# A chunked recurrence beside attention: first products that wait for a whole group, and PSUM banks split by kind

## The chip, the cores and the metric

The kernel runs on one core of a Trainium2 chip. The metric is the device time of one execution in microseconds (us). The engines of the core are TensorE (PE; its weight loads are listed as PEld), VectorE (DVE), ScalarE (ACT), GpSimd (POOL) and SyncE (SP), which issues nearly all transfers. Each engine works through its own queue in order; semaphores tie the queues together.

## The reference, cut to what matters

One layer of a backbone with two parallel head groups on 1024 latent and 256 context tokens: differential attention (8 heads) and an RWKV-7 recurrence over 16 heads of size 64 in both directions. Their gated outputs go through one output projection and a final norm.

```python
def step(S, inp):                      # S: heads x value x key
    r_t, w_t, k_t, v_t, kk_t, b_t = inp
    sa = jnp.einsum('bhvk,bhk->bhv', S, -kk_t)
    S = S * w_t[:, :, None, :] + sa[..., None] * b_t[:, :, None, :] + v_t[..., None] * k_t[:, :, None, :]
    return S, jnp.einsum('bhvk,bhk->bhv', S, r_t)

# attention, for each block of 128 queries
p = jax.nn.softmax(s, axis=-1)         # two maps, m = 0 and 1
a = p[:, :, 0] - lam * p[:, :, 1]
o = jnp.einsum('bhqk,bkhv->bqhv', a, v)
```

## The kernel before

A first phase computes the input projection and writes its results to scratch tensors in HBM; the change doesn't touch it. The function `mix_phase` does the rest: the recurrence, the attention and the output projection run side by side, and after the recurrence's end the tail finishes attention and projection.

The recurrence is computed in chunks of 32 tokens (`CH`). One step of the outer loop, a tick, is one chunk for four pairs of heads in both directions. There are 80 ticks: ten items (a group of four pairs times five segments of 256 tokens) of eight chunks. Two chunks (`HN`) make a part, so there are 40 parts. The four pairs are handled as two duos `w`. For each duo and for odd and even parts there is a buffer `L` (left operands) and `R` (right operands: state, values and a solved part).

A tick in `step` is: first products (line 893) into PSUM, which are copied (line 901) into rows 96 to 128 of `R`; state products (line 913), which are multiplied with the decay (line 924) into the next chunk's state rows of `R`; output products (line 936), which are copied (line 939) into `ys` and stored to HBM by `store_y` (line 953). Duo `w` has bank `bank[w]`, with columns 0 to 128 for the first products, 128 to 256 for the outputs and 256 to 512 for the states. After the first products comes `fill(0)`, after the outputs `fill(1)`: these calls put attention work and, a piece each, the norms, the projections and the next item's inverse into the program.

`load_part` loads the operands of a later part when the part two before it has been read: L<-kt (line 772), R<-vb (781), L<-ra (782), and the inverse Tb<-td (793). `prep` (products at 803, copies at 806) multiplies the loaded operands with the inverse and writes the result into rows 96 to 128 of `L`; it is written in the second tick of the part before, for one duo after the other, through one bank `yb`. The inverse itself is computed by `inverse` on POOL (lines 734 and 736), from `aw`, and goes to HBM as `td`.

Attention is a generator: `scores` (1057, 1060) writes negated score blocks and running minima, an exponential follows the last block (1068), `weight` (1074, 1075) and `combine` (1081) mix the two maps, `trans` (1089, 1091) transposes and `values` (1104) multiplies with the values. PSUM tiles for the scores and the transposes have two buffers each. `norm` (980 to 1007) normalises the recurrence's outputs, `load_wo` (1247 to 1251) loads and splits the projection's weights, `project` (1275 to 1300) multiplies.

The order of the instructions on each engine isn't that of the program. A planner simulates the program, and whenever an engine is free it takes, of what is ready by its own estimate, the instruction that is earliest in the program; inside `tc.high_priority(offset=n)` an instruction counts as n places earlier. That order is then fixed, and on the chip every engine keeps to it. Before, only the copies at 901 and the multiplications at 924 have an offset (`HPC = 500`).

Of the kernel before, what the change touches and what calls it, by code (L numbers as in the profile page):

```python
# [34 lines left out]
NC = SEG // CH  # L35
HN = 2
# [11 lines left out]
YBUF = 1  # L48
# [14 lines left out]
HPY = 0  # L63
# [677 lines left out]
def mix_phase(ctx, tc, i, o, s, ident, nhalf, dram, td0, neglam, subg, lnh, heads, psm):  # L741
# [94 lines left out]
    bank = [psx.tile([P, 512], F32, name=f"bank{w}") for w in duos]  # L836
# [18 lines left out]
    def start_item(w, m):  # L855
# [6 lines left out]
        px = bank[w]  # L862
# [18 lines left out]

    def step(j, k, fill):
# [4 lines left out]
        for w in duos:  # L887
            L, R = slots[w, j % 2]
            for d in range(2):
                for e in range(2):  # L890
                    for h in range(2):
                        u = 64 * e + 32 * h
                        nc.tensor.matmul(bank[w][u:u + 32, 64 * d:64 * d + 64], L[0:96, e, h, d, k, 96:128],
                                         R[0:96, k, d, e, hv(h)], start=True, stop=True, tile_position=(0, u))
        with ahead(HPC):
            for w in duos:
                R = slots[w, j % 2][1]
                for e in range(2):
                    for h in range(2):
                        u = 64 * e + 32 * h  # L900
                        (nc.vector.tensor_copy if w else nc.scalar.copy)(  # L901
                            R[96:128, k, :, e, hv(h)], bank[w][u:u + 32, 0:128].rearrange("p (d v) -> p d v", d=2))
        later_prep = k == HN - 1 and j + 1 < n_part
        if later_prep:
            prep(j + 1, 0, yb)
        fill(0)
        for w in duos:
            L, R = slots[w, j % 2]
            for e in range(2):
                for d in range(2):  # L910
                    for h in range(2):
                        o_ = 256 + 128 * d + 64 * e
                        nc.tensor.matmul(bank[w][hv(h), o_:o_ + 64], L[:, e, h, d, k, 0:64],  # L913
                                         R[:, k, d, e, hv(h)], start=True, stop=True, tile_position=(0, 64 * h))
        with ahead(HPC):
            for w in duos:
# [6 lines left out]
                for h in range(2):  # L923
                    nc.vector.tensor_tensor(dst[:, :, :, hv(h)], bank[w][hv(h), 256:512].rearrange("p (d e v) -> p d e v", e=2, d=2),  # L924
                                            wcs[p0][hv(h), 2 * w:2 * w + 2, sg + 1, :, c:c + 1].rearrange("p e d o -> p d e o").broadcast_to([HD, 2, 2, HD]), op=ALU.mult)
        g = c // 4
        if c % 4 == 0:
            ysb[m, g] = cp.tile([P, 4, NL, HD], F32, tag="ys", name=f"ys{m}_{g}", bufs=YBUF)
        for w in duos:
            L, R = slots[w, j % 2]  # L930
            for e in range(2):
                o_ = P + 64 * e
                for h in range(2):
                    for d in range(2):
                        q = 64 * d + 32 * h
                        nc.tensor.matmul(bank[w][q:q + 32, o_:o_ + 64], L[:, e, h, d, k, 64:96], R[:, k, d, e, hv(h)],  # L936
                                         start=True, stop=True, tile_position=(0, q))
        for w in duos:
            nc.scalar.copy(ysb[m, g][:, c % 4, 2 * w:2 * w + 2], bank[w][:, P:2 * P].rearrange("p (e v) -> p e v", e=2))
        if later_prep:  # L940
            prep(j + 1, 1, yb)
# [101 lines left out]
    def attention():  # L1043
# [128 lines left out]
        for n in range(NB + 2):  # L1172
# [25 lines left out]
            if pp is not None:  # L1198
                vp = [(pp, c) for c in range(1 if len(st[pp]["ch"]) > 1 else 0, len(st[pp]["ch"]))]
# [348 lines left out]
```

## Time and profile before

| what | value |
|---|---|
| median of three runs | 2613.61 us (2607.57 to 2620.56) |
| the profiled execution | 2612.43 us |
| its span, first to last instruction | 2610.6 us |
| mean granted TensorE clock | 0.943 |
| TensorE busy | 2363.7 us |

The profile is that of one execution. For each group of instructions of a line it has the busy time, the mean duration and what ended the idle time before them; for each engine it lists who it waited for. A timeline row gives start and length of neighbouring instructions of one line, merged. The granted clock is given as a share of 2.4 GHz; TensorE has two levels, 2.4 and 1.2 GHz. Starting times are counted from the span's start. The mixed phase begins at about 1230 us; the recurrence's products run until about 2383 us.

### The profile page before, as it was taken

The numbers are of one execution on the slowest core, as the hardware profiler recorded it, in microseconds if no ns is written. First come the engines' busy times: TensorE is split into PE (matmuls) and PEld (weight loads), VectorE is DVE, ScalarE is ACT, GpSimd is POOL, SyncE is SP. The second block draws the span as 40 slices with busy tenths as digits, with TensorE's granted clock in tenths as the row PEclk, the third lists the DMA queues.
The fourth block names the chain that finished last, engine by engine and source line by source line (L and its number), as shares of the span: only waits on it lengthen the run. The fifth ranks groups of instructions, "written<-read, shape, count | busy, mean of one in ns | idle before, by whom it ended". The sixth has DMA issues, their size and how long they took to land.

```text
span 2610.6 us, 60873 instructions
## 1 busy us (share of the span) xinstructions
PE 2363.7 (91%) x23907; PEld 1902.6 (73%) x23907; DVE 1559.8 (60%) x3210; ACT 1192.9 (46%) x2606; POOL 1166.5 (45%) x1725
## 2 busy tenths in 40 slices
PE   6999999999999999898698989898989998898796
PEld 4888888888888888787466767676766676776674
DVE  5656565555455655533566877685745565576558
ACT  3334443334334343331466666574545554564342
POOL 4234343243433342465446666556647311043564
PEclk9999999999999999998799999897988998999898
DMA  7465656565646564567978887877887888787445
GB/s 240 108 157 134 178 143 181 139 164 161 155 128 161 135 180 120 165 167 165 225 156 166 163 163 146 165 150 169 167 200 183 211 191 190 176 222 207 148 146 181
DMA packets 516734, 437.56 MB, mean 168 GB/s; under 512 B 156552, under 2 KB 460852, under 8 KB 511329
## 3 DMA queue, kind: packets, MB, share of 16 engines
q1 hardware_dynamic: 514352, 427.94, 66.8%
q0 software_dynamic: 2096, 5.75, 1.2%
q8 instruction: 188, 3.08, 0.5%
q14 instruction: 98, 0.79, 0.1%
HBM read 258.69 MB, written 163.86 MB: 162 GB/s over the span
## 4 chain that ended last, share of the span: by engine, by line
PE 55%; DMA 19%; DVE 8%; POOL 6%; SPq 5%; issue 3%; ACT 2%; POOLq 0%; DVEq 0%; ACTq 0%
DMA L<-kt 5%; PE sc L1057 5%; PE po L1104 4%; PE bank L913 3%; PE pa L1089 3%; PE yb L803 3%; PE pg L449 3%; DMA acc<-acc 2%; PE pso L1298 2%; DMA wst<-w_out 2%; PE pso L1299 1%; DMA Tb<-td 1%; PE pso L1300 1%; PE bank L936 1%; PE psg_v L335 1%
## 5 line engine op out<-in xcount | busy, mean ns | idle before, releaser
L1057 PE MATMUL sc<-ka,q 128*128 128x512 f32 (+1 forms) x832 | 302.3, 452 | 17.5 <-DVE pb L1060 9.3
L1060 DVE TENSOR_SCALAR_CACHE_REDUCE pb<-sc,mn 128x512 f32<-128x512 f32 x256 | 191.6, 749 | 112.2 <-PE sc L1057 104.4
L1068 ACT ACTIVATE pb<-pb,mn 128x1536 f32<-128x1536 f32 (+1 forms) x160 | 218.4, 1365 | 75.3 <-DVE pb L1060 74.5
L734 POOL TENSOR_TENSOR tmp<-aw,tt 128x31 f32<-128x31 f32 (+15 forms) x310 | 163.4, 527 | 168.9 <-DMA aw<-kt 67.8
L1104 PE MATMUL po<-vk,aT 128*128 128x128 f32 x1600 | 237.2, 289 | 0.9 <-ACT aT L1091 0.7
L1104 PEld LDWEIGHTS po<-vk,aT 128*128 128x128 f32 x1600 | 217.2, 201 | 17.2 <-ACT aT L1091 1.4
L479 POOL TENSOR_SCALAR ta<-ta,ka 128x256 f32<-128x256 f32 x80 | 81.1, 1014 | 292.8 <-DVE bk L477 292.7
L456 ACT COPY km<-ptk 64x256 f32<-64x256 f32 x320 | 117.4, 367 | 182.3 <-PE ptk L453 160.4
L736 POOL TENSOR_TENSOR tt<-tt,tmp 128x31 f32<-128x31 f32 (+15 forms) x310 | 180.8, 583 | 18.2
L803 PE MATMUL yb<-L,Tb 32*32 32x96 f32 x2496 | 105.3, 269 | 81.1 <-DMA L<-kt 59.5
L806 ACT COPY L<-yb 32x384 f32<-32x384 f32 x312 | 146.3, 469 | 67.9 <-PE yb L803 63.8
L1057 PEld LDWEIGHTS sc<-ka,q 128*128 128x128 f32 x832 | 137.8, 201 | 53.6 <-DVE pb L1060 20.1
L1081 DVE SCALAR_TENSOR_TENSOR pb<-pb,cc,pb 128x512 f32<-128x512 f32 (+1 forms) x208 | 167.8, 856 | 2.0
L1091 ACT COPY aT<-pa 128x512 f32<-128x512 f32 (+1 forms) x208 | 116.2, 570 | 104.0 <-PE pa L1089 102.2
L924 DVE TENSOR_TENSOR R<-bank,wc 64x256 f32<-64x256 f32 x312 | 130.9, 420 | 54.6 <-PE bank L913 45.3
L450 DVE TENSOR_TENSOR km<-pg,msk 128x512 f32<-128x512 f32 x80 | 55.1, 688 | 175.7 <-PE pg L449 147.0
L1089 PE MATMUL pa<-ident,pb 128*128 128x128 f32 x800 | 137.7, 297 | 17.6 <-DVE acc L1292 10.4
L803 PEld LDWEIGHTS yb<-L,Tb 32*32 32x32 f32 x2496 | 66.3, 114 | 116.2 <-issue 42.2
L1060 DVE TENSOR_SCALAR_CACHE_REDUCE pb<-sc 128x512 f32<-128x512 f32 (+1 forms) x160 | 101.3, 636 | 80.7 <-PE sc L1057 67.8
L913 PEld LDWEIGHTS bank<-R,L 128*64 128x64 f32 x2560 | 102.2, 152 | 49.1 <-issue 20.5
L913 PE MATMUL bank<-R,L 128*64 128x64 f32 x2560 | 126.2, 244 | 8.3 <-ACT R L901 4.3
L1089 PEld LDWEIGHTS pa<-ident,pb 128*128 128x128 f32 x800 | 97.2, 150 | 45.1 <-DVE acc L1292 13.1
(354 smaller groups left out, 6496.2 us busy)
## 6 DMA issues: line engine op xcount, KB each, us to landing
kt<-km SPq DMA_DIRECT2D x160, 256.0 KB
L<-kt SPq DMA_DIRECT2D x80, 512.0 KB
acc<-acc SPq DMA_DIRECT2D x50, 512.0 KB
ra<-ra SPq DMA_DIRECT2D x160, 128.0 KB
L<-ra SPq DMA_DIRECT2D x80, 256.0 KB
R<-vb SPq DMA_DIRECT2D x160, 64.0 KB
y<-ys SPq DMA_DIRECT2D x80, 128.0 KB
yn<-y SPq DMA_DIRECT2D x40, 256.0 KB
```

The source lines that it names most:

```text
L734: e.tensor_tensor(mv, aw[:n, t, t + 1:CH].unsqueeze(2).broadcast_to([n, w, j]), tt[:n, t:t + 1, 0:j].broadcast_to([n, w, j]), op=ALU.mult)
L736: e.tensor_tensor(tt[:n, t + 1:CH, 0:j], tt[:n, t + 1:CH, 0:j], mv, op=ALU.add)
L803: nc.tensor.matmul(pp[32 * q:32 * q + 32, n:n + 96], Tb[96:128, e, HN * q + c, :], L[96:128, e, q // 2, q % 2, c, 0:96], start=True, stop= ...
L806: nc.scalar.copy(L[96:128, :, q // 2, q % 2, :, 0:96], pp[32 * q:32 * q + 32, 0:192 * HN].rearrange("p (e c y) -> p e c y", e=2, y=96))
L913: nc.tensor.matmul(bank[w][hv(h), o_:o_ + 64], L[:, e, h, d, k, 0:64], R[:, k, d, e, hv(h)], start=True, stop=True, tile_position=(0, 64 * h))
L924: nc.vector.tensor_tensor(dst[:, :, :, hv(h)], bank[w][hv(h), 256:512].rearrange("p (d e v) -> p d e v", e=2, d=2), wcs[p0][hv(h), 2 * w:2 ...
L1057: nc.tensor.matmul(sc, q[:, v, m, qc], ka[:, m, 0:kn], start=(v == 0), stop=(v == 1))
L1060: nc.vector.tensor_scalar(pm[:, c * 512:c * 512 + kn], sc, -0.125, mn[:, c - 1:c] if c else None, op0=ALU.mult, op1=ALU.min, accum_out=mn[ ...
L1068: nc.scalar.activation(v, v, AF.Exp, bias=mn[:, c:c + 1], scale=-1.0, accum_out=B["l"][:, m, B["b"]:B["b"] + 1])
L1081: nc.vector.scalar_tensor_tensor(a, B["p"][1][:, v], B["cc"], a, op0=ALU.mult, op1=ALU.add)
L1089: nc.tensor.transpose(pt[:, t * P:(t + 1) * P], B["p"][0][:, 512 * c + t * P:512 * c + (t + 1) * P], ident)
L1104: nc.tensor.matmul(po, B["aT"][c][:, t * P:(t + 1) * P], vk[:, t, :], start=(c == 0 and t == 0), stop=(c == last and t == nt - 1))
```

## The change

In `step` the banks are split by kind: `bank[0]` takes the first products of both duos (columns 0 to 256) and the outputs of both (256 to 512), `bank[1]` the states of both. The copies into `R` become four of 32x256 on ACT instead of eight of 32x128 on ACT and DVE; the copy of the outputs becomes one of 128x256. `hold` collects the instructions that make a group's operands, and `held` ties the first product of the group to all of them. All products of the recurrence, `prep` included, now stand inside the offset of 500. `ys` holds one part instead of two, in two buffers, and is stored after every part.

Beside this, the exponential is put into the program an item of attention later, `weight` and `combine` move into the next block, all of a block's `values` come two blocks later, the inverses run as one chain that is paced over the ticks and begins four ticks earlier (`INVA`), attention starts two ticks later (`LEAD`), two operations of `norm` move from POOL to DVE, and `load_wo` keeps two loads ahead of the split.

```diff
+INVA = 4
+LEAD = 2
-YBUF = 1
+YBUF = 2
-HPY = 0
+HPY = 500
...
-    bank = [psx.tile([P, 512], F32, name=f"bank{w}") for w in duos]
+    bank = [psx.tile([P, 512], F32, name=f"bank{n}") for n in range(2)]
...
+    whole = []
+
+    def hold(x):
+        whole.append(x.ins.name)
+
+    def held(x):
+        for y in whole:
+            tc.add_manual_dep(x.ins, y, mybir.DependencyInfo(mybir.DependencyClass.Sync, mybir.DependencyReason.DATA))
+        whole.clear()
+
     def step(j, k, fill):
...
+        with ahead(HPC):
             for d in range(2):
                 for e in range(2):
-                    for h in range(2):
-                        u = 64 * e + 32 * h
-                        nc.tensor.matmul(bank[w][u:u + 32, 64 * d:64 * d + 64], L[0:96, e, h, d, k, 96:128],
-                                         R[0:96, k, d, e, hv(h)], start=True, stop=True, tile_position=(0, u))
+                    for w in duos:
+                        L, R = slots[w, j % 2]
+                        for h in range(2):
+                            u, o_ = 64 * w + 32 * h, 128 * d + 64 * e
+                            x = nc.tensor.matmul(bank[0][u:u + 32, o_:o_ + 64], L[0:96, e, h, d, k, 96:128],
+                                                 R[0:96, k, d, e, hv(h)], start=True, stop=True, tile_position=(0, u))
+                            held(x)
+            for w in duos:
+                R = slots[w, j % 2][1]
+                for h in range(2):
+                    u = 64 * w + 32 * h
+                    hold(nc.scalar.copy(R[96:128, k, :, :, hv(h)],
+                                        bank[0][u:u + 32, 0:256].rearrange("p (d e v) -> p d e v", d=2, e=2)))
+            if later_prep:
+                prep(j + 1, 0, yb)
+        fill(0)
         with ahead(HPC):
             for w in duos:
-                R = slots[w, j % 2][1]
+                L, R = slots[w, j % 2]
                 for e in range(2):
-                    for h in range(2):
-                        u = 64 * e + 32 * h
-                        (nc.vector.tensor_copy if w else nc.scalar.copy)(
-                            R[96:128, k, :, e, hv(h)], bank[w][u:u + 32, 0:128].rearrange("p (d v) -> p d v", d=2))
...
+                    for d in range(2):
+                        for h in range(2):
+                            o_ = 256 * w + 128 * d + 64 * e
+                            x = nc.tensor.matmul(bank[1][hv(h), o_:o_ + 64], L[:, e, h, d, k, 0:64],
+                                                 R[:, k, d, e, hv(h)], start=True, stop=True, tile_position=(0, 64 * h))
+                            held(x)
...
+        with ahead(HPY):
+            for w in duos:
...
+                            nc.tensor.matmul(bank[0][q:q + 32, o_:o_ + 64], L[:, e, h, d, k, 64:96], R[:, k, d, e, hv(h)],
+                                             start=True, stop=True, tile_position=(0, q))
+            nc.scalar.copy(ysb[m, g][:, k], bank[0][:, 256:512].rearrange("p (x v) -> p x v", x=NL))
+            if later_prep:
+                prep(j + 1, 1, yb)
         fill(1)
...
-        yield
-        yield
+        for _ in range(4):
+            yield
...
-        nc.gpsimd.tensor_tensor(y[0], y[0], y[1], op=ALU.add)
-        yield
-        yield
+        nc.vector.tensor_tensor(y[0], y[0], y[1], op=ALU.add)
...
+            soon.append(lambda: nc.scalar.activation(v, v, AF.Exp, bias=mn[:, c:c + 1], scale=-1.0,
+                                                     accum_out=B["l"][:, m, B["b"]:B["b"] + 1]))
...
+            for c in range(max(nk, len(vq))):
+                if c < nk:
+                    yield item(scores, cost, n, 0, c)
+                if c == 2 and cb:
+                    combine(p, cb.pop(0))
+                if c < len(vq):
+                    yield item(values, 0.87, *vq[c])
+                if c == 1 and cb:
+                    weight(p)
+                    combine(p, cb.pop(0))
...
+                if len(got) == 2:
+                    split()
                 c = slice(n * 512, n * 512 + 512)
                 w = op.tile([P, 512], F32, tag="wst", name=f"wst{nm}_{k}_{n}", bufs=2)
                 nc.sync.dma_start(w, i["w_out"][0, sl[k]:sl[k] + P, c])
...
-            if state["inv"] is not None:
-                for _ in range(2):
-                    next(state["inv"], None)
+            while state["ninv"] < 33 * (state["t"] + INVA + _ / 4 + pos / 2) / NC:
+                next(state["inv"], None)
+                state["ninv"] += 1
...
+    state["inv"], state["ninv"] = inverses(), 0
+    state["credit"] = -LEAD * total / n_tick
...
-        if c % 4 == 3:
-            at(t + 1, lambda m=m, g=c // 4: store_y(m, g))
+        if k == HN - 1:
+            at(t + 1, lambda m=m, g=c // HN: store_y(m, g))
```

## Rows read from the trace of the kernel before

**Rows 1.** the page, busy us of each engine, share of span, instructions

```profile
PE 2363.7 (91%) x23907; PEld 1902.6 (73%) x23907; DVE 1559.8 (60%) x3210; ACT 1192.9 (46%) x2606; POOL 1166.5 (45%) x1725
```

**Rows 2.** windows, both stages: us, PE, PEld, DVE, ACT, POOL busy, PEclk, DMA, GB/s

```profile
1290.00:2383.00 1093.00, 975.19 (x13236) 746.39 (x13236) 711.45 (x1795) 633.37 (x1520) 537.40 (x967) 0.91 0.82 176
2383.00:2611.00 228.00, 179.45 (x860) 138.74 (x856) 151.09 (x303) 80.39 (x169) 121.49 (x149) 0.92 0.51 170
```

**Rows 3.** waits of PE, 1230 to 2612 us; total us, times, longest

```profile
PE yb L803 <- DMA L<-kt: 59.5, 23, 10.4
PE yb L803 <- DMA Tb<-td: 15.2, 4, 8.3
PE pso L1298 <- ACT ohi L1281: 12.8, 5, 5.8
PE pa L1089 <- DVE acc L1292: 10.4, 6, 5.3
PE sc L1057 <- DVE pb L1060: 9.3, 17, 1.5
...
PE bank L936 <- DVE R L924: 6.8, 11, 2.9
PE bank L893 <- ACT ys L939: 6.1, 4, 2.4
PE pa L1089 <- DVE pb L1081: 5.9, 10, 1.1
PE bank L913 <- ACT R L901: 4.3, 8, 1.0
PE bank L913 <- DVE R L901: 3.6, 6, 0.9
```

**Rows 4.** groups by line, 1230 to 2612 us; count, busy us, mean ns, idle

```profile
L806 ACT COPY L<-yb 32x384 f32<-32x384 f32 x312 | 146.3, 469 | 67.9 <-PE yb L803 63.8
...
L901 DVE COPY R<-bank 32x128 f32<-32x128 f32 x320 | 92.6, 289 | 44.4 <-PE bank L893 36.9 <-PE bank L936 1.4 <-ACT aT L1091 1.0
L901 ACT COPY R<-bank 32x128 f32<-32x128 f32 x320 | 81.7, 255 | 29.5 <-PE bank L893 25.6
L939 ACT COPY ys<-bank 128x128 f32<-128x128 f32 x160 | 39.8, 266 | 82.8 <-PE bank L936 72.7 <-DMA y<-ys 3.5 <-issue 2.6
...
L987 POOL TENSOR_TENSOR yn<-yn,m 128x256 f32<-128x256 f32 x40 | 25.9, 669 | 9.3 <-DVE m L984 8.3 <-DVE cc L1074 0.9
L980 POOL TENSOR_TENSOR yn<-yn 128x512 f32<-128x512 f32 x20 | 25.8, 1291 | 65.7 <-DMA yn<-y 54.0 <-DVE pb L1060 10.5 <-PE sc L1057 1.2
...
L1372 DVE TENSOR_TENSOR x<-x,y 128x1024 f32<-128x1024 f32 x10 | 16.9, 1690 | 9.8 <-POOL y L1371 9.8
```

**Rows 5.** one line's instructions, L893: duration ns, first and last start

```profile
L893 PE MATMUL bank<-R,L x2560: 216/219/317, 1242.9 to 2379.8; 96*32 96x64 f32 x197
```

**Rows 6.** timeline of PE in one part; start us, length us

```profile
2235.91 0.65 PE L936 MATMUL bank<-R,L 128*32 128x64 f32 x32
...
2238.31 0.65 PE L893 MATMUL bank<-R,L 96*32 96x64 f32 x32
...
2242.11 0.48 PE L803 MATMUL yb<-L,Tb 32*32 32x96 f32 x10 [0.29 <-DMA L<-kt]
```

**Rows 7.** waits of DVE, ACT and POOL, the same stretch

```profile
DVE cc L1074 <- ACT pb L1068: 40.2, 39, 3.9
...
ACT wohi L1250 <- DMA wst<-w_out: 19.6, 11, 4.9
...
POOL yn L980 <- DMA yn<-y: 54.0, 12, 15.1
```

**Rows 8.** timeline of SP's queue in the same part

```profile
2236.76 0.47 SPq L772 DMA_DIRECT2D L<-kt  x1
2237.32 2.05 SPq L953 DMA_DIRECT2D y<-ys  x4
2239.42 0.50 SPq L772 DMA_DIRECT2D L<-kt  x1
```

More of the change, by code (lines that the diff above doesn't have):

```diff
@@ L904, in step @@
[L904 to L914, printed above, removed]
@@ L923, in step @@
                 for h in range(2):
[L924 to L941, printed above, removed]
+                    hold(nc.vector.tensor_tensor(dst[:, :, :, hv(h)], bank[1][hv(h), 256 * w:256 * w + 256].rearrange("p (d e v) -> p d e v", e=2, d=2),
+                                                 wcs[p0][hv(h), 2 * w:2 * w + 2, sg + 1, :, c:c + 1].rearrange("p e d o -> p d e o").broadcast_to([HD, 2, 2, HD]), op=ALU.mult))
+        g = c // HN
+        if k == 0:
+            ysb[m, g] = cp.tile([P, HN, NL, HD], F32, tag="ys", name=f"ys{m}_{g}", bufs=YBUF)
+        with ahead(HPY):
+            for w in duos:
+                L, R = slots[w, j % 2]
+                for e in range(2):
+                    o_ = 256 + P * w + 64 * e
+                    for h in range(2):
+                        for d in range(2):
+                            q = 64 * d + 32 * h
+                            nc.tensor.matmul(bank[0][q:q + 32, o_:o_ + 64], L[:, e, h, d, k, 64:96], R[:, k, d, e, hv(h)],
[3 more added lines that the diff above has]
+                prep(j + 1, 1, yb)
         fill(1)
@@ L1063, in scores @@
                 return
[L1064 to L1068 removed]
+            v = pm[:, 0:kn * nk]
+            soon.append(lambda: nc.scalar.activation(v, v, AF.Exp, bias=mn[:, c:c + 1], scale=-1.0,
+                                                     accum_out=B["l"][:, m, B["b"]:B["b"] + 1]))
         def weight(n):
@@ L1247, in load_wo @@
                 nc.sync.dma_start(w, i["w_out"][0, sl[k]:sl[k] + P, c])
-                if g is not None:
-                    nc.gpsimd.tensor_tensor(w, w, g[:, c], op=ALU.mult)
-                nc.scalar.copy(whi[:, k, c], w)
-                nc.gpsimd.tensor_tensor(wlo[:, k, c], w, whi[:, k, c], op=ALU.subtract)
-                if n:
-                    yield
+                got.append((w, k, c))
+                yield
+        while got:
+            split()
+        yield
     def project(j):
@@ L1419, in fill, with inverses @@
             turn(projs)
+    def inverses():
+        for b in range(1, n_item):
+            yield from invert(b)
+            yield
+    state["inv"], state["ninv"] = inverses(), 0
+    state["credit"] = -LEAD * total / n_tick
     for t in range(n_tick):
```

74 lines of the change are left out of this document (33 added, 41 removed).

## The prediction

> **What bounds the kernel now.** I read the busy shares first. TensorE is busy 91% of the span [rows 1], and the change leaves its matmuls in number and shape as they are; so it can only win time in which TensorE stands still, and time that it runs at half clock because it stood still. The windows say where: the stretch before the mixed phase is untouched by the diff, so everything happens after 1230 us. In the recurrence stage (1290 to 2383 us, 1093.0 us) TensorE is busy 975.2 us, so 117.8 us are idle, at a mean granted clock of 0.91; in the tail 228.0 us hold 179.5 us [rows 2]. With two levels of the clock (2.4 and 1.2 GHz), 0.91 means that 18% of the stage, 197 us, ran at the lower one. If all the idle time lay in those 197 us, 79 us of work would still have run at half speed, a loss of some 40 us. So an idle microsecond carries about 40/117.8 = 0.34 us of lost clock with it; I price each one at 1.34 (estimate).
>
> Third, who is waited for [rows 3]. The ten rows, 133.9 us, fall in three heaps. The product that folds the inverse into the next part's operands (`prep`, L803) waits 59.5 us in 23 places for the transfer L<-kt and 15.2 us in 4 for Tb<-td: over half. The recurrence's own products (L893, L913, L936) wait 6.8 + 6.1 + 4.3 + 3.6 = 20.8 us. Attention and output projection wait 12.8 + 10.4 + 9.3 + 5.9 = 38.4 us. So the chain that the change's title names is the smallest heap.
>
> **The change part by part.**
>
> *Banks by kind, outputs next to states.* The output products L936 wait for the vector engine's L924 (6.8 us), although they read nothing it writes: both use one bank. In the new layout outputs share bank 0 with the first products, and L924 reads bank 1, so this wait goes. L893 waits for the copy of the outputs (6.1 us); the outputs now come earlier in the tick, but the first products still share a bank with them, and now with those of both duos: I take 4 of 6.1. Together -10.8 us.
>
> The Trainium skill, "PSUM — Partial Sum Buffer", section "PSUM bank collisions raise a hardware error", says that engines are to be kept apart by bank and quadrant, not by address. The trace agrees as far as L936 behind L924 goes, 6.8 us, and by the rule that term is the same as by the row. The same rule speaks against the change at the next products: both duos' first products wait for one copy of 128x256, and by it the sum would be worse by what that copy leaves uncovered.
>
> That copy is not in the trace. 128x128 takes 266 ns [rows 4]; twice that, 532 ns, is the upper end for 128x256, for 80 ticks 43 us if nothing covers it. What covers it is the attention of the second `fill`, which lies between: 80 ticks take 1242.9 to 2379.8 us [rows 5], 14.2 us each, and the chain in one is short: a group of products 0.65 us [rows 6], the state group about twice that (estimate), copies 1.5, updates 1.7, some 5 us. I take nothing, 43 us stays an end.
>
> *Four copies, all on the scalar engine.* Before, four 32x128 copies of 255 ns ran on ACT (1.02 us) beside four of 289 ns on DVE (1.16 us) [rows 4]. Now four 32x256 run on ACT. Between 255 ns (32x128) and 469 ns (32x384) [rows 4] a 32x256 lies at 362 ns: 1.45 us, some 0.3 to 0.4 us later than the later of the two. The state products L913 wait for these copies in 14 places [rows 3]; 14 x 0.3 is +4 us; if all 80 ticks showed it, 80 x 0.4 = 32 us. I take +4. DVE gives up 92.6 us of copies; ACT pays 320 x 0.362 = 116 for 81.7, and saves some of L939's 39.8 us. Neither engine bounds the stage.
>
> *The first product of a group waits for all.* Two duos' updates are four L924 of 420 ns, 1.7 us, before anything starts, where half of it let the first duo go. Queued behind the waiting product on TensorE are the attention products of the next `fill`. No row of TensorE has L893 waiting for DVE, so the update is in time today; at worst 80 x 0.84 = 67 us, below nothing it can't be. I take 0: what makes room is that outputs no longer stand between the state products and the update.
>
> Recurrence: -10.8 + 4 = -7 us.
>
> *Exp, weight and combine a block later.* DVE stands 40.2 us in 39 places for the exponential [rows 7], and the score reductions queue behind. TensorE's waits for that engine are 9.3 us (L1057) and 5.9 us (L1089) [rows 3]. I take two thirds, -10 us; ends 0 and -15.2. The 10.4 us of L1089 behind L1292 come from a transfer of acc and stay.
>
> *Weights two loads ahead.* ACT stands 19.6 us for wst<-w_out [rows 7] with the copies that feed TensorE queued behind. TensorE's row for that neighbour, L1298 behind ohi, is 12.8 us; I take -4, ends 0 and -12.8.
>
> *Inverses spread, four ticks ahead.* At best the 15.2 us of Tb<-td go. But the first item's inverse isn't moved, and the transfer itself stays: I take a quarter, -4.
>
> *Norm's sums on DVE.* POOL loses 25.8 + 25.9 us (L980, L987). On DVE a 128x1024 tensor_tensor takes 1.69 us [rows 4]; by columns 20 x 0.85 + 40 x 0.42 = 34 us, less than the 92.6 us it gave up. What moves too is the wait for yn<-y, 54.0 us in 12 places on POOL [rows 7]: on DVE, the state updates and score reductions stand behind it. The add is now written four yields behind its load instead of two, so I take 0, and keep 54 us as an end.
>
> *Loads and stores of a part.* The operands' buffer is free when the last output product has read it. A part's rows show the order: L936 at 2235.91, prep at 2242.11 after 0.29 us of waiting [rows 6]; L<-kt issued at 2236.76, then four stores y<-ys for 2.05 us, and only then the second L<-kt at 2239.42 [rows 8]. Outputs right behind the states issue these loads earlier, by up to the 1.7 us of the update. Some of that time becomes slack for prep: I take a fifth of the 59.5, -12 us. The stores come at every part instead of every second: 20 more batches of 2.05 us on SP's queue, in front of one of the loads, 41 us if the second prep were on the edge; I take 0, since the trace's waits fall on the first prep.
>
> The Trainium skill, "DMA: Bandwidth & Descriptors", section "Rules for kernel authors", warns of transfers under 64 KB and advises joining small ones; the change halves the stores to that size. The rows show only the issue time; the rule alone would change no term, since nothing on the chain waits long for the stores.
>
> Sum: -7 - 10 - 4 - 4 - 12 = -37 us idle, times 1.34 = -50 us. The profiled execution took 2612.4 us, within 1.2 us of the median. Forecast 2562 us; own range 2525 to 2597, from the ends that are nearest to the rows.
>
> *The lead.* Attention starts two ticks late, the recurrence ends earlier by about as much, and the tail gets what attention was left out. TensorE is 89% busy in the stage and 79% in the tail [rows 2]: moving two ticks' attention (some 16 us) costs 16 x 0.1 = 2 us, left out.
>
> **The rivals.**
>
> *The transfer takes it back.* Prep waits for L<-kt; if the DMA engines, 0.82 busy in the stage [rows 2], pace the parts, what TensorE saves elsewhere it waits longer there. For it: the largest row of the waits is this. Against: 23 waits, while 39 parts with two preps each pass. Only some 7 us of the sum stay: 2612 - 7 x 1.34 = 2603; 2597 to 2622.
>
> *Slower: prep too early.* Both preps move under the priority of 500, where they had none. TensorE's order is fixed before the run, and if prep is put sooner behind its load, TensorE stands before it with all attention queued behind. Price: in the part shown prep starts 5.35 us after the issue [rows 6, 8]; if it came straight behind the first products (2238.96) it would wait 3.1 us longer, 39 x 3.1 = 121 us. At half, 39 x 1.55 x 1.34 = 81 us: 2562 + 81 = 2643; at the whole 2724. It decides from 37/39 = 0.95 us a part. For it: the waits say that prep already arrives before its data. Against: it already stands well ahead of where the step writes it, so priority may be no longer what holds it.
>
> *More: the loads come in time.* If the earlier issue clears half of the 59.5 us instead of a fifth, 18 us x 1.34 = 24 us more, and the other terms at their better ends (-6 recurrence, -5 attention, -9 weights) 27 more: 2511; 2470 to 2525.
>
> *The groups are not kept whole.* The wait stands on the first product only; attention may still be ordered between the others. Then the recurrence's -7 is lost: 2571, inside the forecast.
>
> **How the numbers follow.** Forecast 0.46; taken back 0.20; prep too early 0.20; more 0.14. The range should leave out 2 in 10: below 2500 some 0.07, above 2640 some 0.11. A measurement of this kernel tells about 0.5%, 13 us, from no change: faster means below 2600.5. That is the forecast, the larger gain and a quarter of the second case, 0.65; within it 0.15; slower 0.20.
>
> **What would show it.** Right: L936 no longer waits for L924; no DVE wait for the exponential; ACT's wait for wst gone; L803's wait for L<-kt at 40 to 60 us; idle in the stage near 85 us and the granted clock at 0.93 or above. Wrong: L803's waits above 100 us (prep too early); L803 near 60 with nothing else left and the span unmoved (taken back); DVE waiting for yn<-y by tens of us with L893 behind DVE.

## The result and the profile after

The changed kernel takes 2899.56 us in the median (2893.28 to 2912.26, four runs) where the kernel before, run beside it, takes 2616.98 us: a ratio of 1.111, 95% interval 1.107 to 1.115. The forecast was 2562 us, the range 2500 to 2640. It is 11% slower, and outside of every case that the prediction named: the slowest of them was priced at 2724 us.

The page of the changed kernel, busy us of the engines:

```profile
PE 2751.5 (95%) x23907; PEld 2156.8 (75%) x23907; DVE 1477.8 (51%) x2950; ACT 1224.6 (42%) x2528; POOL 1130.1 (39%) x1665
```

TensorE has the 23907 matmuls of [rows 1], and yet 387.8 us more of busy time (2751.5 for 2363.7). Its idle time has *fallen*, from 246.9 to 139.8 us of the span. The span's growth is the sum of the two: 387.8 - 107.1 = 280.7 us (2891.3 for 2610.6).

The window of the changed kernel's recurrence stage, columns as in [rows 2]:

```profile
1290.00:2634.00 1344.00, 1322.74 (x13188) 969.18 (x13188) 624.55 (x1511) 656.53 (x1426) 497.98 (x902) 0.98 0.63 141
```

In the stage TensorE is busy 1322.7 of 1344.0 us, at a granted clock of 0.98 instead of 0.91. Neither idle time nor the clock is the cause.

Waits of TensorE in the mixed phase, total us, times, longest, to be held against [rows 3]:

```profile
PE sc L1069 <- DVE pb L1072: 18.0, 15, 4.6
...
PE yb L805 <- DMA Tb<-td: 4.9, 3, 4.2
```

The row that led before, 59.5 us for L<-kt, is gone; Tb<-td is down from 15.2 to 4.9. What the prediction hoped for in prep's waits came, and more. The time went elsewhere. Groups of TensorE in the mixed phase (count, busy us, mean ns, idle before):

```profile
L926 PE MATMUL bank<-R,L 128*64 128x64 f32 x2560 | 429.3, 250 | 6.7 <-ACT R L914 5.9
L950 PE MATMUL bank<-R,L 128*32 128x64 f32 x2560 | 390.0, 235 | 0.0
...
L805 PE MATMUL yb<-L,Tb 32*32 32x96 f32 x2496 | 88.3, 253 | 5.7 <-DMA Tb<-td 4.9 <-DMA R<-vb 0.4 <-ACT L L808 0.4
L907 PE MATMUL bank<-R,L 96*32 96x64 f32 x2560 | 62.1, 227 | 3.4 <-issue 1.8 <-DVE R L937 1.1
```

L926 are the state products, L950 the outputs, L805 is prep. The same view of the kernel before, with the states as L913, the outputs as L936 and prep as L803:

```profile
L913 PE MATMUL bank<-R,L 128*64 128x64 f32 x2560 | 126.2, 244 | 8.3 <-ACT R L901 4.3 <-DVE R L901 3.6
...
L803 PE MATMUL yb<-L,Tb 32*32 32x96 f32 x2496 | 105.3, 269 | 81.1 <-DMA L<-kt 59.5 <-DMA Tb<-td 15.2 <-DMA y<-ys 3.4
...
L936 PE MATMUL bank<-R,L 128*32 128x64 f32 x2560 | 72.8, 235 | 7.0 <-DVE R L924 6.8
```

Before, the 2560 instructions of either group were busy 126.2 and 72.8 us. Now it is 429.3 and 390.0 us, while the first products (L907) and prep cost no more than they did. The mean of one instruction, 250 and 235 ns, has hardly moved (244 and 235 before). So one instruction takes as long as ever; what is lost is that neighbours ran side by side. The timeline of the changed kernel shows it (start us, length us, count of merged instructions):

```profile
1515.86 0.30 PE L950 MATMUL bank<-R,L 128*32 128x64 f32 x2
1516.09 0.33 PE L926 MATMUL bank<-R,L 128*64 128x64 f32 x2
1516.35 0.30 PE L950 MATMUL bank<-R,L 128*32 128x64 f32 x2
1516.58 0.33 PE L926 MATMUL bank<-R,L 128*64 128x64 f32 x2
1516.83 0.30 PE L950 MATMUL bank<-R,L 128*32 128x64 f32 x2
```

An output product (32 columns wide), a state product (64 columns wide), an output product, and so on; each product is two instructions. A round of one each takes 0.49 us (1515.86, 1516.35, 1516.83), 16 rounds are a tick: 7.8 us. Before, by the groups' busy time, (126.2 + 72.8)/80 = 2.5 us. 80 ticks x 5.3 us = 424 us; TensorE's busy time grew by 388, since that of other groups fell meanwhile, prep's by 17.0 us (105.3 to 88.3).

### The profile page after: what moved, and what is told of

The parts are those of the page before. It is cut to its first block, busy times and chain, and to the rows that moved or that the text cites. A ratio compares the mean times of both kernels' runs of the same rounds, so it can differ in the third digit from the quotient of the medians.

```text
span 2891.3 us, 60416 instructions
## 1 busy us (share of the span) xinstructions
PE 2751.5 (95%) x23907; PEld 2156.8 (75%) x23907; DVE 1477.8 (51%) x2950; ACT 1224.6 (42%) x2528; POOL 1130.1 (39%) x1665
## 4 chain that ended last, share of the span: by engine, by line
PE 75%; DMA 7%; DVE 6%; POOL 5%; SPq 3%; ACT 3%; issue 2%; POOLq 0%; DVEq 0%; ACTq 0%
PE bank L926 12%; PE bank L950 10%; PE sc L1069 6%; PE po L1114 5%; PE pa L1099 3%; PE pg L451 3%; PE yb L805 2%; PE pso L1322 2%; PE pso L1324 2%; PE pso L1323 2%; PE bank L907 1%; PE ptk L455 1%; PE psg_v L338 1%; PE psg_v L336 1%; PE psg_v L337 1%
## 5 line engine op out<-in xcount | busy, mean ns | idle before, releaser
L926 PE MATMUL bank<-R,L 128*64 128x64 f32 x2560 | 429.3, 250 | 6.7 <-ACT R L914 5.9
L950 PE MATMUL bank<-R,L 128*32 128x64 f32 x2560 | 390.0, 235 | 0.0
L926 PEld LDWEIGHTS bank<-R,L 128*64 128x64 f32 x2560 | 250.2, 138 | 146.5 <-issue 20.8
L1069 PE MATMUL sc<-ka,q 128*128 128x512 f32 (+1 forms) x832 | 285.4, 435 | 18.9 <-DVE pb L1072 18.0
L950 PEld LDWEIGHTS bank<-R,L 128*32 128x32 f32 x2560 | 178.4, 109 | 92.8 <-issue 4.3
L952 ACT COPY ys<-bank 128x256 f32<-128x256 f32 x80 | 29.8, 372 | 464.6 <-PE bank L950 444.0
L1114 PE MATMUL po<-vk,aT 128*128 128x128 f32 x1600 | 223.4, 282 | 1.0 <-ACT aT L1101 1.0
L1114 PEld LDWEIGHTS po<-vk,aT 128*128 128x128 f32 x1600 | 206.2, 195 | 15.4 <-ACT aT L1101 1.8
L736 POOL TENSOR_TENSOR tmp<-aw,tt 128x31 f32<-128x31 f32 (+15 forms) x310 | 163.4, 527 | 126.2 <-DMA y<-ys 35.5
L1306 POOL TENSOR_TENSOR olo<-of,ohi 128x512 fp32r<-128x512 f32 x30 | 38.9, 1296 | 266.5 <-ACT ohi L1305 216.3
```

Of the source, the lines that this page charges most:

```text
L736: e.tensor_tensor(mv, aw[:n, t, t + 1:CH].unsqueeze(2).broadcast_to([n, w, j]), tt[:n, t:t + 1, 0:j].broadcast_to([n, w, j]), op=ALU.mult)
L926: x = nc.tensor.matmul(bank[1][hv(h), o_:o_ + 64], L[:, e, h, d, k, 0:64], R[:, k, d, e, hv(h)], start=True, stop=True, tile_position=(0, ...
L950: nc.tensor.matmul(bank[0][q:q + 32, o_:o_ + 64], L[:, e, h, d, k, 64:96], R[:, k, d, e, hv(h)], start=True, stop=True, tile_position=(0, q))
L1069: nc.tensor.matmul(sc, q[:, v, m, qc], ka[:, m, 0:kn], start=(v == 0), stop=(v == 1))
L1114: nc.tensor.matmul(po, B["aT"][c][:, t * P:(t + 1) * P], vk[:, t, :], start=(c == 0 and t == 0), stop=(c == last and t == nt - 1))
```

## The experiments

The theory that this suggests: the two groups now have the same rank for the planner, since both stand under an offset of 500 and are ready at once; it takes them in turn, and a change of the tile's shape between neighbours (the rows by columns of TensorE that a product takes) keeps them from running side by side. Each ratio is to the kernel before, run beside that experiment (2607 to 2611 us in the median).

**The outputs ranked behind.** One constant, which is also the offset of prep's second half, written behind the outputs:

```diff
-HPY = 500
+HPY = 450
```

> The changed kernel with one constant changed: the offset of the output products is 450 instead of 500, so that the planner ranks all of a tick's outputs behind all of its state products. Theory A: the changed kernel is slower because state and output products have equal rank and go out one by one in turn, so that neighbours no longer run side by side. Then the two groups' busy time, 429.3 and 390.0 us, falls back to near 126 and 73 us; TensorE's busy sum fell short of that by 388 us before, so the time is 2900 - 388 = 2512 us, plus what idle time comes back (107 us less idle in the changed kernel than before): 2512 to 2620 us. Theory B: the split of the banks or the wait of the first product for the whole group costs the time itself; then it stays above 2800 us.

2662.6 us, ratio 1.020 (1.016 to 1.025). 237 us of the loss are gone with that constant, so the rank is the cause of most of it; but 2662 lies above the 2620 that theory A allows. The reason is in the groups of this kernel's mixed phase, and in its timeline behind 1519 us:

```profile
L805 PE MATMUL yb<-L,Tb 32*32 32x96 f32 x2496 | 146.0, 267 | 87.8 <-DMA Tb<-td 39.3 <-DMA L<-kt 37.8 <-ACT aT L1101 4.3
...
L950 PE MATMUL bank<-R,L 128*32 128x64 f32 x2560 | 111.2, 237 | 0.0
L926 PE MATMUL bank<-R,L 128*64 128x64 f32 x2560 | 108.4, 240 | 6.1 <-ACT R L914 5.9
```

The timeline:

```profile
1519.99 0.53 PE L805 MATMUL yb<-L,Tb 32*32 32x96 f32 x2
1520.44 0.42 PE L950 MATMUL bank<-R,L 128*32 128x64 f32 x2
1520.79 0.52 PE L805 MATMUL yb<-L,Tb 32*32 32x96 f32 x2
```

State products are down to 108.4 us. Now it is prep (L805) whose products come two instructions at a time, 0.8 us apart (at a granted clock of 0.50 here), with an output product between them: 146.0 us of busy time for 105.3. Both are 32 columns wide, but one has 32 rows and the other 128: a change of rows keeps neighbours apart too. The offset that takes one group out of step with another puts it in step with a third.

**The same order, one shape.** The output products take 64 columns instead of 32:

```diff
-  nc.tensor.matmul(bank[0][q:q + 32, o_:o_ + 64], L[:, e, h, d, k, 64:96], R[:, k, d, e, hv(h)],
-                   start=True, stop=True, tile_position=(0, q))
+  nc.tensor.matmul(bank[0][hv(h), o_:o_ + 64], L[:, e, h, d, k, 32:96], R[:, k, d, e, hv(h)],
+                   start=True, stop=True, tile_position=(0, 64 * h))
```

> The changed kernel, but each output product takes 64 columns of the left operand instead of 32 and writes to the same column half of the array as the state product ahead of it; the outputs of the recurrence are wrong by that. The order stays one by one in turn between the two banks, but all products of the two groups now have one shape. Theory A1 (the change of shape between neighbours is what keeps them apart): a round of one state and one output product falls from 488 ns towards 2 x 99 ns = 198 ns, 16 rounds x 80 ticks x 0.29 us = 371 us less, about 2530 us and up to 100 us more where idle time returns. Theory A2 (going from bank to bank or from group to group keeps them apart whatever the shape): the round stays near 490 ns and the time near 2900 us.

2627.4 us, ratio 1.006 (1.003 to 1.009). The products still stand in turn, mostly one by one, and still in two banks; half of the outputs take the column half of the state product ahead of them. The page's busy shares and two groups, and a piece of the timeline:

```profile
PE 2363.7 (90%) x23907; PEld 1957.7 (74%) x23907; DVE 1486.0 (56%) x2950; ACT 1225.5 (46%) x2528; POOL 1135.9 (43%) x1665
...
L949 PE MATMUL bank<-R,L 128*64 128x64 f32 x2560 | 192.3, 235 | 0.0
L926 PE MATMUL bank<-R,L 128*64 128x64 f32 x2560 | 191.5, 237 | 10.6 <-ACT R L914 10.5
```

The timeline, where outputs are now L949:

```profile
1699.80 0.23 PE L926 MATMUL bank<-R,L 128*64 128x64 f32 x2
1699.86 0.22 PE L949 MATMUL bank<-R,L 128*64 128x64 f32 x1
1699.86 0.22 PE L926 MATMUL bank<-R,L 128*64 128x64 f32 x1
1699.92 0.23 PE L949 MATMUL bank<-R,L 128*64 128x64 f32 x2
```

TensorE's busy time is 2363.7 us, that of the kernel before, though each output product has become wider. Neighbours start 0.06 us apart. A1 holds: it is the change of the tile's shape that keeps neighbours apart, not the change of bank or group. Busy time fell by 387.8 us where 371 were expected, and 132.4 us of idle time came back (139.8 to 272.2 us of the span), somewhat more than the 100 us that were allowed for.

**In turns of four.** States and outputs in one block, four products of one kind, four of the other (in the innermost loops of `step`):

```diff
             for w in duos:
                 for e in range(2):
                     for d in range(2):
                         for h in range(2):
                             ... (state product)
+                    for h in range(2):
+                        for d in range(2):
+                            ... (output product)
```

> The changed kernel with state and output products written in one block in turns of four products each, so that there are 8 changes between the groups in a tick instead of 32. Theory A: a round of one each costs 488 ns where contiguous groups take 99 + 57 = 155 ns (126.2 and 73 us over 1280 products), so a change costs (488 - 155)/2 = 167 ns; 8 changes are 1.3 us a tick, 107 us over the contiguous order, and 4 x 107 = 427 us over it with 32 changes. So this kernel lies 80 to 110 us above the one with the outputs behind, about 2610 to 2720 us. If the loss goes with the loss of neighbours on other columns rather than with each change, four in a row run side by side and it lies within 40 us of that one.

2615.0 us, ratio 1.002 (1.000 to 1.005): 48 us *below* the kernel with the offset at 450, where 80 to 110 above it was expected. In its groups the states are busy 158.6 us (108.4 there) and the outputs 110.2 (111.2), but prep only 86.3 (146.0 there): the comparison was spoiled by prep; it is made again, with prep the same in both, at the end.

**All but the recurrence.** The step, its banks, offsets and stores as before, the other parts of the change kept:

```diff
-YBUF = 2
+YBUF = 1
-HPY = 500
+HPY = 0
-    bank = [psx.tile([P, 512], F32, name=f"bank{n}") for n in range(2)]
+    bank = [psx.tile([P, 512], F32, name=f"bank{w}") for w in duos]
...
```

> The step of the recurrence, its banks, its offsets and its stores as before; all the rest of the change kept: exponential, weight and combine later, inverses paced, attention two ticks later, two sums of the norm on DVE, weights two loads ahead. By the prediction's terms for these parts (-10, -4, -4 us of TensorE's waits, times 1.34) about 2617 - 24 = 2593 us. If the sums of the norm carry their wait for yn<-y to DVE, or attention's start two ticks later leaves a hole, 2640 us or more; then some of the loss has nothing to do with the order of the products.

2590.5 us, ratio 0.993 (0.991 to 0.995); 2593 was expected. So the rest of the change is a small gain, and the loss is all in the recurrence. The waits behind the number are another matter:

```profile
DVE cc L1073 <- ACT pb L1066: 32.5, 29, 4.4
...
DVE yn L982 <- DMA yn<-y: 30.0, 14, 6.1
...
ACT wohi L1252 <- DMA wst<-w_out: 24.1, 14, 4.8
...
PE sc L1058 <- DVE pb L1061: 18.1, 18, 5.4
...
PE yb L805 <- DMA Tb<-td: 10.3, 2, 6.8
...
PE pso L1311 <- ACT ohi L1294: 8.9, 3, 3.6
```

DVE still waits 32.5 us for the exponential (40.2 before, [rows 7]), ACT 24.1 us for the weights (19.6), TensorE 18.1 us for the score reductions (9.3, [rows 3]). The wait for yn<-y did move to DVE, 30.0 us of it. Two of TensorE's waits fell as forecast: for Tb<-td from 15.2 to 10.3, for ohi from 12.8 to 8.9 ([rows 3]).

**One block, and prep out of the offset.** In the first of these two the outputs are written right behind the states in one block under the offset; in the second prep is also taken out of the offset, both of its calls as here:

```diff
-            if later_prep:
-                prep(j + 1, 0, yb)
+        if later_prep:
+            prep(j + 1, 0, yb)
```

> The changed kernel, the outputs written right behind the state products inside the same offset of 500, so that no output can rank with a state product. In the kernel with the outputs' offset at 450 the products of prep (32x32) still stood in turn with the outputs (128x32): their busy time was 146.0 us where the kernel before has 105.3, and the outputs' 111.2 where it has 72.8. In this order, too, a part of the outputs stands in turn with prep, though less. Theory A (each change of shape between neighbours costs): between 2590 us (the rest of the change alone) and 2662 us (offset 450), about 2620, with prep's busy time between 105 and 146 us. Theory B (the new layout of the recurrence costs by itself): no less than 2650 us.

> As the kernel with one block, and prep's products stand outside of the offset again, as they did before. Theory A: all groups are whole; prep's busy time is back at 105 us, the outputs' at 73. The prediction's term for the recurrence (-7 us, times 1.34) on top of the rest of the change alone gives 2590 - 9 = 2581 us. Theory B (four copies on ACT, one wait for the whole group and one bank for both duos cost by themselves): 2610 us or more with the waits of the state products for the copies and of the first products for the updates grown by tens of us.

2661.8 us (ratio 1.022, 1.021 to 1.024) and 2577.9 us (0.989, 0.986 to 0.991). The first lies at the upper end of theory A and inside theory B; the second decides for A, with the states' wait for the copies at 15.4 us. Taking prep's two calls out of the offset is worth 84 us. In the first kernel, busy shares and groups:

```profile
PE 2411.6 (91%) x23907; PEld 1938.6 (73%) x23907; DVE 1488.4 (56%) x2950; ACT 1223.1 (46%) x2528; POOL 1134.7 (43%) x1665
...
L805 PE MATMUL yb<-L,Tb 32*32 32x96 f32 x2496 | 135.5, 274 | 75.5 <-DMA L<-kt 43.4 <-DMA Tb<-td 28.5 <-issue 3.2
...
L929 PE MATMUL bank<-R,L 128*64 128x64 f32 x2560 | 130.2, 244 | 9.5 <-ACT R L914 9.5
...
L939 PE MATMUL bank<-R,L 128*32 128x64 f32 x2560 | 89.9, 242 | 4.4 <-issue 4.4
```

Its timeline, where prep stands in turn with attention's 128x128 products:

```profile
1603.44 0.35 PE L805 MATMUL yb<-L,Tb 32*32 32x96 f32 x2
1603.72 0.49 PE L1114 MATMUL po<-vk,aT 128*128 128x128 f32 x2
1604.14 0.35 PE L805 MATMUL yb<-L,Tb 32*32 32x96 f32 x2
```

In the second kernel, busy shares and groups:

```profile
PE 2326.3 (91%) x23907; PEld 1892.1 (74%) x23907; DVE 1484.9 (58%) x2950; ACT 1222.8 (48%) x2528; POOL 1138.4 (44%) x1665
...
L929 PE MATMUL bank<-R,L 128*64 128x64 f32 x2560 | 117.5, 238 | 16.3 <-ACT R L914 15.4 <-ACT L L808 0.9
...
L805 PE MATMUL yb<-L,Tb 32*32 32x96 f32 x2496 | 99.9, 263 | 55.0 <-DMA Tb<-td 44.6 <-DMA L<-kt 6.3 <-ACT acc L1314 1.3
...
L939 PE MATMUL bank<-R,L 128*32 128x64 f32 x2560 | 79.6, 232 | 0.4 <-issue 0.4
```

Busy time falls by 85.3 us (2411.6 to 2326.3), most of the 92.9 us that lie between the spans of the two profiled executions. 35.6 of it are prep's (135.5 to 99.9), 12.7 the states' (130.2 to 117.5) and 10.3 the outputs' (89.9 to 79.6); the rest is spread over the other groups, beside a better clock (0.934 to 0.951 in the mean). The prediction's own sum for the recurrence, 2590.5 - 7 x 1.34 = 2581 us, lies within 4 us of what is measured once the groups stay whole; that is luck in part, since its terms came out otherwise (see below). The second kernel takes 1.1% less than the one before (0.9 to 1.4%).

**No offset on any product.** The outputs stand behind the updates again, and the copies and updates alone keep the offset:

```diff
-HPY = 500
+HPY = 0
-        with ahead(HPC):
+        if True:
             for d in range(2):
...
+        with ahead(HPC):
             for w in duos:
                 R = slots[w, j % 2][1]
...
-        with ahead(HPC):
+        if True:
             for w in duos:
                 L, R = slots[w, j % 2]
```

> The changed kernel with no offset on any product of the recurrence, as before; the copies and the multiplications keep theirs, banks by kind, four copies and the wait of the first product stay. Theory A: whole groups, 2581 us as above, within 15 us of the kernel with prep outside of the offset: the rank ahead of attention is worth little by itself. If the rank matters (products that come late hold the loads of the next part), it lies 20 us or more above that one.

2576.6 us (0.989, 0.987 to 0.991), the same. Neither the rank ahead of attention nor the earlier place of the outputs brings anything that shows.

**The inverse's buffer.** In the kernel with prep outside of the offset prep waits 44.6 us for Tb<-td and 6.3 us for L<-kt (its line L805 above). Now the loaded inverse lies in two buffers of half the size, one for each duo, each with a transfer of its own:

```diff
-        Tb = cp.tile([P, NL, 4 * HN, CH], F32, tag="Tb", name=f"Tb{j}", bufs=TBUF)
+        for w in duos:
+            Tb = cp.tile([P, 2, 4 * HN, CH], F32, tag="Tb", name=f"Tb{j}_{w}", bufs=2)
...
```

> The kernel with prep outside of the offset (2578 us), and the loaded inverse lies in two buffers, one for each duo, instead of one for both, in the same space; each is loaded by its own transfer of half the size. In that kernel prep waits 44.6 us in 16 places for Tb<-td, which is issued only when the last prep has read the one buffer, and 6.3 us for L<-kt. Theory C (the outputs' earlier end frees the operands L in time, and the wait is now for the one buffer of the inverse): Tb<-td falls by half or more, some 25 us of idle time, 2545 to 2570 us. Rival (another transfer takes its place, or 40 more transfers of half the size are late themselves): the waits of prep stay at 50 us or more and the time within 10 us of 2578.

2586.7 us (0.992, 0.989 to 0.995). The wait for Tb<-td falls to 18.5 us, L<-kt rises to 21.1 (waits of TensorE in its mixed phase):

```profile
PE yb L806 <- DMA L<-kt: 21.1, 5, 7.9
PE yb L806 <- DMA Tb<-td: 18.5, 3, 9.5
```

The two rows together lose 11.3 us of 50.9, and two of attention's waits gain 8.9 and 4.8 (from 19.1 and 17.9). So theory C had the wait for Tb<-td right (26.1 us less) and the time wrong: no time is won, as the rival said, though prep's waits fell to 39.6 us where it had 50 or more. That the time was lost to attention's waits is read from the rows and not shown.

**Eight copies on two engines, and no wait for the group**, each in the kernel with prep out of the offset:

```diff
-                    hold(nc.scalar.copy(R[96:128, k, :, :, hv(h)],
+                    for e in range(2):
+                        hold((nc.vector.tensor_copy if w else nc.scalar.copy)(
+                            R[96:128, k, :, e, hv(h)],
...
```

> The kernel with prep outside of the offset (2578 us), with eight copies of 32x128 instead of four of 32x256, those of the second duo on DVE, as before the change. The prediction priced the four copies on ACT at +4 us of TensorE's waits, 0 to 32. In that kernel the state products wait 15.4 us in 10 places for these copies. If the four copies cost what the prediction says, 2573 us; if nearly all of the 15.4 us are theirs, 2560 us; if the 92 us that DVE takes back weigh more, 2585 us or above.

```diff
     def held(x):
-        for y in whole:
+        for y in ():
```

> The kernel with prep outside of the offset (2578 us) without the added dependencies: the first product of a group waits for its own operands only, as every product does. The prediction priced the wait for the whole group at 0, at worst 67 us, and never a gain. If the wait keeps groups whole in the planned order, then without it parts of groups come apart, there are more changes of shape on TensorE, and this kernel is 10 us or more slower; if it costs, it is up to 10 us faster; else within 10 us.

2594.3 us (0.993, 0.991 to 0.996) and 2594.2 us (0.995, 0.992 to 0.997), against 0.989 (0.986 to 0.991). Four copies on ACT cost nothing that shows; going back to eight lies on the slow side. There prep's waits for L<-kt and Tb<-td are 61.2 and 21.8 us for 6.3 and 44.6, the states' wait for DVE's copies is 12.4 us, and TensorE's busy time is lower (2305.5 us): what costs there are prep's waits, and what moved them stays open. Without the group's wait TensorE's busy time is higher by 45.8 us. The page's busy shares, and the timeline of a group of first products (L907):

```profile
PE 2372.1 (91%) x23907; PEld 1916.3 (74%) x23907; DVE 1482.5 (57%) x2950; ACT 1221.7 (47%) x2528; POOL 1139.2 (44%) x1665
```

The timeline:

```profile
1506.68 0.30 PE L907 MATMUL bank<-R,L 96*32 96x64 f32 x2
1506.91 0.49 PE L1114 MATMUL po<-vk,aT 128*128 128x128 f32 x2
1507.33 0.30 PE L907 MATMUL bank<-R,L 96*32 96x64 f32 x2
```

Here first products stand in turn with attention's. In the groups the states are busy 134.8 us and prep 117.0, where they are 117.5 and 99.9 with the wait. So the wait earns its keep, some 16 us in the medians: with it the groups stand together. The prediction had excluded a gain there.

**The order alone.** In the kernel without any offset on a product, states and outputs are written in one loop, one by one in turn (n = 1), and in turns of four (n = 4); the updates follow:

```diff
+            ss = [(e, d, h) for e in range(2) for d in range(2) for h in range(2)]
+            oo = [(e, d, h) for e in range(2) for h in range(2) for d in range(2)]
+            for q0 in range(0, 8, n):
+                for e, d, h in ss[q0:q0 + n]:
+                    ... (state product)
+                for e, d, h in oo[q0:q0 + n]:
+                    ... (output product)
```

> The kernel without an offset on any product (2577 us), with state and output products written one by one in turn. Theory A: the order alone, with no rank involved, brings the loss back: a round of one each 488 ns instead of 155, 16 rounds x 80 ticks x 0.333 = 426 us at most, less what TensorE's idle time (172 us) gives way; the changed kernel had 388 us more busy and 107 us less idle time, so +281: about 2860 us, 2820 to 2900. If the rank ahead of attention was a part of the loss, it stays below 2800 us.

> The same in turns of four products each. The first kernel in turns of four, with all products of the recurrence under the offset, took 2615 us, but prep was under the offset there too. If a loss goes with each change of shape, 8 changes a tick cost a quarter of what 32 cost: 2577 + 70 = 2647 us (by 2860 for 32). If it goes with the loss of a neighbour on other columns, four in a row lose only at their ends: 2577 to 2610 us.

2907.6 us (1.114, 1.108 to 1.121) and 2622.1 us (1.007, 1.003 to 1.010). The first lies just above the expected range, the second between the two forecasts, 2647 us and 2577 to 2610. The first is the changed kernel's time, and its groups are the changed kernel's groups, with no product's rank involved (L930 states, L936 outputs):

```profile
PE 2768.9 (95%) x23907; PEld 2160.2 (74%) x23907; DVE 1484.5 (51%) x2950; ACT 1223.6 (42%) x2528; POOL 1127.9 (39%) x1665
...
L930 PE MATMUL bank<-R,L 128*64 128x64 f32 x2560 | 435.8, 254 | 5.4 <-ACT R L915 5.3
L936 PE MATMUL bank<-R,L 128*32 128x64 f32 x2560 | 395.6, 238 | 0.0
```

In turns of four the page and the same groups are

```profile
PE 2408.1 (92%) x23907; PEld 1927.3 (74%) x23907; DVE 1485.9 (57%) x2950; ACT 1224.2 (47%) x2528; POOL 1132.3 (43%) x1665
...
L930 PE MATMUL bank<-R,L 128*64 128x64 f32 x2560 | 167.5, 249 | 8.2 <-ACT R L915 8.1
...
L936 PE MATMUL bank<-R,L 128*32 128x64 f32 x2560 | 116.4, 243 | 0.0
```

The page of the kernel that both are held against, without an offset on any product:

```profile
PE 2325.7 (90%) x23907; PEld 1889.6 (73%) x23907; DVE 1486.4 (58%) x2950; ACT 1220.5 (47%) x2528; POOL 1134.5 (44%) x1665
```

Against its 2576.6 us, turns of one cost 331 us and turns of four 46 us. In a tick the first have 31 changes of shape, the second 7, whole groups 1: 30 and 6 more. That is 331/(30 x 80) = 0.14 us for a change, and 46/(6 x 80) = 0.10 us. In TensorE's busy time (2768.9 and 2408.1 against 2325.7 us) the two agree: 443.2/2400 = 0.18 and 82.4/480 = 0.17 us. So each change costs much the same, and the time shows less of it where idle time gave way (250.8 us of the span in the kernel held against, 211.7 in turns of four, 136.0 in turns of one). (The kernel held against has the updates between the two groups, the two others behind both; the kernel with prep out of the offset has them behind both too and takes the same 2578 us.)

## Why the prediction was wrong

*The step that failed* is in its first paragraph: the change "leaves its matmuls in number and shape as they are; so it can only win time in which TensorE stands still". Number and shape did stay. Their order didn't, and busy time depends on it: it rose by 387.8 us with the order of the changed kernel, by 443.2 us with that order alone, and was back at 2363.7 us with the same order in one shape. The view for it had been there: 2560 instructions of L913 with a mean of 244 ns would be 625 us one after the other, and the group's busy time was 126 us. A group whose busy time is a fifth of its count times its mean lives off its neighbours, and a change that moves its neighbours has to be priced for that.

*The rank.* The prediction priced the outputs' move as relief and looked for whom they would wait. That they could stand *between* the state products was seen only for attention ("the groups are not kept whole", 2571 us), at the price of a lost term of 7 us. Before the change the shared bank prevented it: a duo's outputs waited for its L924 and so for all of its states. The split of the banks took away the wait of 6.8 us and with it what kept the order; the offset then put the two in turn, since without it, in the same banks, they stay apart (2576.6 us).

The Trainium skill, "TensorEngine Tiling (Array Packing)", section "Key Properties", says that changing the tiling mode drains TensorE. The trace agrees: with one tile shape the same order is back at the busy time before, 2363.7 us. By that rule the change would have been among the rivals; the page gives no price, the rows do, 331 us.

*The terms.* Banks: the wait of the outputs for the updates is gone, as said; the first products still wait 6.1 us for the copy of the outputs in the kernel with prep out of the offset, where 4 us of it were to go. Copies: the state products' wait for them is 15.4 us in the kernel with whole groups, +7.5 instead of +4. The whole group's wait: taken at 0 with a gain excluded, it is a gain of 16 us (2594.2 to 2577.9). So the recurrence's 2581 us were met by terms that do not make them up. Loads: -12 us were taken for L<-kt; in that kernel it fell from 59.5 to 6.3, and Tb<-td rose from 15.2 to 44.6, so prep's waits went from 74.7 to 50.9. With eight copies it was back at 61.2; what decides it is open. The rival "the transfer takes it back" was right in part, by another transfer than its own. The norm on DVE was left at 0 with 54 us as an end: 30.0 us of the wait for yn<-y did come to DVE, and TensorE's wait for the score reductions rose from 9.3 to 18.1 us; whether by that, no run shows. The rest of the change: 2593 by the sum and 2590.5 measured, and that is luck. Two of the three waits went as said (-3.9 for ohi, -4.9 for Tb<-td), though ACT's own wait for the weights, which was to bring the first, rose from 19.6 to 24.1 us. The largest went the other way: TensorE's wait for the score reductions was to fall and rose by 8.8 us. TensorE's idle time stayed (248.4 for 246.9 us of the span), and its busy time fell by 15.2 us. Which part did that is open; no run took them apart, and none shows the factor of 1.34 on idle time.

*The slower rival* named the right place, prep under the offset, and the wrong mechanism. Its price was waiting for L<-kt, 81 us at half. Prep under the offset cost 84 us, nearly all as busy time, since its products stood in turn with others; its waits for L<-kt and Tb<-td were 71.9 us there and 50.9 without. That the two prices nearly agree is luck.

*What is open:* why the planner takes two groups of one rank in turn. If an offset only counted places in the program, the states, written first, would still come first; no run shows how it ranks them. That it takes them in turn is shown by the changed kernel; that the time follows from the order and not from the rank is shown by the kernel in turn without an offset.

## What to carry to other kernels

Compare a group's busy time with its count times its mean: where it is a fraction, the group runs side by side, and its order on the engine is a term of the sum like any other. Keep products of one tile shape together when ranks or banks are changed, since a wait that is removed may have been what kept them so. An offset in priority moves a group into step with whatever stands that far ahead; ranks that tie are to be looked for.

## What the runs showed of the hardware

A float32 product of 32 or 64 columns costs by what stands next to it: 16 state and 16 output products take 2.5 us as whole groups (the phase's mean in the kernel before) and 7.8 us in turn (at a granted clock of 1.00), and the mean of one instruction is the same. The tile's shape decides, not the bank: products of 128 rows and 64 columns from two banks, in turn, start 0.06 us apart, those of 64 and 32 columns 0.23 to 0.26 us. At 32 columns, products of 32 and 128 rows in turn also stay apart, 0.35 to 0.45 us at a granted clock of 0.50. Not every change costs: between first products (96 rows, 32 columns) and outputs (128 rows, 32 columns) the next start came after 0.03 us in the median of 61 places in the kernel before. TensorE's granted clock was 0.98 in the stage in which such turns kept it 98% busy, and 0.91 before, where it was idle for 11%.
